# A hybrid encoder step on one core: adaLN weights by feature ahead of x, and the first three projection blocks begun on two thirds of the tokens

## The chip, the cores and the metric

The kernel runs on one core of one Trainium2 chip. The metric is device time in microseconds (us) of one launch. TensorE (PE) multiplies matrices and writes into PSUM, which has eight banks of 128 partitions by 512 float32. VectorE (DVE), ScalarE (ACT) and GpSimd (POOL) do the elementwise work, and SyncE (SP) issues nearly all transfers. Each engine works through its own instructions in the order in which the program wrote them.

## The reference

One layer of a streaming encoder is applied to 1024 prompt tokens and 32 sample tokens, 1056 tokens of 1024 features in all, each of the two sequences with its own conditioning vector c:

```
mod = silu(c) @ w_ada + b_ada                   # 6 x 1024 values; shift 1, scale 1 are the first 2048
h   = rmsnorm(x, g_mix) * (1 + scale1) + shift1
u   = h @ w_in                                  # 5640 columns: q, k, v of 8 heads x 64, the mLSTM's parts, gates
ya  = softmax(q k^T / 8 + rel_bias) v           # in bands of 64-token chunks; the sample also sees a cache
ym  = mlstm(conv(qm, km), vm, om, i, f)
x   = x + gate1 * ((sigmoid(ga) * (ya @ w_br_att) + sigmoid(gm) * (ym @ w_br_mlstm)) @ w_out)
x   = x + gate2 * swiglu(rmsnorm(x, g_ffn) * (1 + scale2) + shift2)
y   = rmsnorm(x, g_final)
```

Outputs are y and the new k, v, convolution and mLSTM states. All inputs are float32.

## The kernel before

Features lie on the partitions and tokens along the free dimension, in 8 tiles h[0..7] of 128 features by 1056 tokens. The tokens are cut into three tiles of 352. A float32 number is held as a rounded high part and the rest as a low part, and each product is three matmuls: weights high times h high, weights low times h high, weights high times h low (`PASSES`, line 41). One projection block is 128 columns of w_in: 3 token tiles x 8 feature tiles x 3 passes = 72 matmuls of 128x128 by 352 columns.

The stage that the change touches is the first one, up to the end of the first head pair's K, V and Q blocks. SP first issues eight tiles of x (128 tokens by 1024 features, 512 KB each, line 220), the sample's tokens, the first 2048 columns of w_ada in eight pieces of 128 rows (1 MB each, line 264), and then the first halves and second halves of two weight blocks, K and V (line 340). x comes token by token, so TensorE transposes it (`x_transposes`, line 281, evicted by ACT on line 282), and DVE sums the squares of each token (line 273). POOL takes the power -1/2 and the result is spread over the partitions as RB.

w_ada comes by rows, that is by the index that is summed over. The scale half of the product goes to TensorE (64 matmuls, line 322). The shift half is summed over rows on DVE (lines 312 and 314) and then over partitions on TensorE (`row_sums`, lines 348 and 352). No scale or shift is known before the last row of w_ada is in.

Then h is made feature tile by feature tile: `scaled_x` (DVE, x * scale * RB), `high_h` (ACT, adds the shift and rounds), `low_h` (DVE, the rest). `first_units` (line 467) runs the K and V blocks side by side over all three token tiles, one h tile after the other, in six PSUM banks, and Q follows as an ordinary block through `unit` (line 436, its matmuls are line 443). K is evicted by lines 553, 556 and 558, V by line 587, Q by lines 640 to 647. While Q runs, V is transposed back to tokens (`v_tail`, line 612) for the attention. After Q come the K, V and Q blocks of the second head pair, with the first pair's attention beside them; from there on the order of the program is the same before and after the change. The rotating pools that matter are `mm` (three PSUM banks), `ps` (psS and psT two banks each, psV one), and `wsp` (four tiles of split weights).

x is also written to a scratch tensor `xres` (line 1508) and read back for the residual. The relative-position bias is spread into a scratch tensor `rb_d` by a 3068 KB transfer (line 672) from which each head's tile is read.

## Time and profile before

| what | value |
|---|---|
| three runs, median | 1598.56 us (1597.11 to 1598.57) |
| profiled execution | 1597.75 us, its span 1596.1 us |
| TensorE busy | 1566.1 us, 98% of the span |
| first matmul of a projection block (line 475) | at 40.97 us |
| first matmul of the second head pair's K (line 443) | at 81.25 us |
| HBM read and written | 153.24 MB and 41.63 MB |

The span runs from the first to the last instruction. 1597.75 - 1596.1 = 1.65 us lie around it. Lines of the timeline give start, duration, engine, line, operation, output<-inputs, and in brackets the idle time of the engine before it and what ended that. Merged lines stand for several instructions in a row (x33).

### The profile page before, as it was taken

How to read it: one execution, taken by the hardware profiler on the slowest of the kernel's cores; microseconds unless marked ns; L12 is line 12 of the kernel's file. 1: busy time of each engine (PE TensorE's matmuls, PEld its weight loads, DVE VectorE, ACT ScalarE, POOL GpSimd, SP SyncE). 2: the span in 40 equal slices, each digit the busy share in tenths (PEclk: the TensorE clock that was granted, in tenths of full speed). 3: DMA queues.
4: the chain of work that ended last, by engine and by line, in shares of the span. 5: the costliest groups of instructions: out<-in, count | busy, mean ns of one | idle time of the engine just before them, and what ended most of it. 6: DMA issues, size and time to landing. Idle time of an engine off the chain costs nothing.

```text
span 1596.1 us, 27244 instructions
## 1 busy us (share of the span) xinstructions
PE 1566.1 (98%) x10167; PEld 1546.2 (97%) x10167; DVE 1126.4 (71%) x2291; ACT 790.5 (50%) x1735; POOL 420.0 (26%) x433
## 2 busy tenths in 40 slices
PE   7999999999999999999999999999999999999997
PEld 6989999999999999999999999999999999999997
DVE  7766555556776845546654699899888886799755
ACT  3665463544555545444433655544544444545443
POOL 0343242433222411000012100565565650000000
PEclk9999999999999999999999999999999999999999
DMA  9823323343132332675443311213222227427444
GB/s 364 265 83 94 98 82 109 86 135 110 43 94 67 88 86 75 133 257 176 133 145 112 106 54 54 95 57 103 81 80 94 68 78 252 143 80 249 130 136 155
DMA packets 209569, 193.48 MB, mean 121 GB/s; under 512 B 11530, under 2 KB 179118, under 8 KB 208414
## 3 DMA queue, kind: packets, MB, share of 16 engines
q1 hardware_dynamic: 206894, 189.92, 38.5%
q8 instruction: 80, 1.31, 0.4%
q10 hardware_dynamic: 2512, 1.77, 0.4%
q14 instruction: 51, 0.42, 0.1%
q0 software_dynamic: 32, 0.06, 0.0%
HBM read 153.24 MB, written 41.63 MB: 122 GB/s over the span
## 4 chain that ended last, share of the span: by engine, by line
PE 91%; DVE 3%; ACT 2%; DMA 2%; issue 1%; SPq 0%; POOL 0%; ACTq 0%; DVEq 0%; POOLq 0%
PE mm L443 41%; PE psb L1811 18%; PE mm L1811 11%; PE psb L2193 3%; PE mm L878 3%; PE mm L2193 2%; PE psV L783 2%; PE psb L2057 2%; PE psS L725 2%; PE psT L752 1%; DMA s<-in_w_ada_dram 1%; PE mm L2057 1%; DMA t<-in_x_sample_dram 1%; PE psV L1112 1%; PE mm L475 1%
## 5 line engine op out<-in xcount | busy, mean ns | idle before, releaser
L443 PE MATMUL mm<-s,wsp 128*128 128x352 f32 x4104 | 687.0, 324 | 0.0
L443 PEld LDWEIGHTS mm<-s,wsp 128*128 128x128 f32 x4104 | 657.3, 188 | 1.8 <-issue 0.4
L410 DVE TENSOR_TENSOR wsp<-wraw,wsp 128x512 fp32r<-128x512 f32 (+1 forms) x280 | 235.6, 858 | 114.1 <-ACT wsp L409 103.1
L1811 PE MATMUL psb<-s,wsp 128*128 128x352 f32 x1611 | 271.7, 322 | 1.6 <-DVE wsp L410 0.9
L409 ACT ACTIVATE wsp<-wraw 128x512 fp32r<-128x512 f32 x336 | 199.5, 617 | 142.4 <-PE psb L1811 44.5
L1811 PEld LDWEIGHTS psb<-s,wsp 128*128 128x128 f32 x1611 | 260.5, 188 | 2.1 <-DVE wsp L410 1.1
L1811 PE MATMUL mm<-s,wsp 128*128 128x352 f32 x933 | 159.3, 322 | 0.0
L1811 PEld LDWEIGHTS mm<-s,wsp 128*128 128x128 f32 x933 | 151.2, 188 | 0.5 <-DVE wsp L410 0.5
L745 POOL TENSOR_SCALAR st<-st,mx 128x640 f32<-128x640 f32 (+5 forms) x72 | 53.1, 738 | 186.2 <-DVE mx L744 171.2
L1207 DVE CUSTOM_DVE_ANT_0 junk<-wa,t 128x512 bf16<-128x512 f32 x128 | 94.7, 740 | 3.1 <-DMA wa<-in_w_mod_dram 2.1
L410 POOL TENSOR_TENSOR wsp<-wraw,wsp 128x512 fp32r<-128x512 f32 x56 | 74.9, 1357 | 57.1 <-ACT wsp L409 55.6
L739 DVE CUSTOM_DVE_ANT_0 st<-psS,bias 128x640 f32<-128x640 f32 (+5 forms) x72 | 44.5, 618 | 57.1 <-PE psS L725 41.9
L740 ACT ACTIVATE st<-st,mx 128x640 f32<-128x640 f32 (+5 forms) x72 | 47.9, 666 | 63.4 <-DVE mx L739 62.3
L1758 POOL TENSOR_TENSOR t<-t,sl 128x352 f32<-128x352 f32 x19 | 18.4, 969 | 212.8 <-ACT sl L1756 212.8
L759 ACT ACTIVATE pT<-psT 128x640 fp32r<-128x640 f32 (+3 forms) x80 | 38.7, 493 | 62.6 <-PE psT L752 47.6
L2166 POOL TENSOR_TENSOR fst<-fst,mhalf 128x6 f32<-128x6 f32 x1 | 2.3, 2312 | 221.1 <-DVE fst L2165 221.1
L764 DVE TENSOR_TENSOR pT<-psT,pT 128x640 fp32r<-128x640 f32 (+3 forms) x80 | 44.0, 558 | 22.2 <-ACT pT L759 22.2
L1420 POOL TENSOR_TENSOR wraw<-wraw,raw 128x512 f32<-128x512 f32 x33 | 55.8, 1705 | 0.9
L878 PE MATMUL mm<-s,s 128*128 128x264 f32 (+3 forms) x432 | 54.5, 283 | 0.0
L2193 PE MATMUL psb<-s,wsp 128*128 128x352 f32 x330 | 54.2, 324 | 0.0
L2193 PEld LDWEIGHTS psb<-s,wsp 128*128 128x128 f32 x330 | 53.1, 188 | 0.1
L878 PEld LDWEIGHTS mm<-s,s 128*128 128x128 f32 (+1 forms) x432 | 52.0, 179 | 0.5
(368 smaller groups left out, 2471.6 us busy)
## 6 DMA issues: line engine op xcount, KB each, us to landing
wraw<-in_w_in_dram SPq DMA_DIRECT2D x38, 512.0 KB, 4.0
wraw<-in_w_gate_up_dram SPq DMA_DIRECT2D x33, 512.0 KB, 3.9
wa<-in_w_mod_dram SPq DMA_DIRECT2D x64, 256.0 KB, 2.8
wraw<-in_w_down_dram SPq DMA_DIRECT2D x32, 512.0 KB, 4.3
a_d<-t SPq DMA_DIRECT2D x22, 528.0 KB, 2.7
g_d<-t SPq DMA_DIRECT2D x16, 528.0 KB, 3.2
x<-xres SPq DMA_DIRECT2D x16, 528.0 KB, 7.1
t<-g_d SPq DMA_DIRECT2D x16, 528.0 KB, 4.5
```

The lines of the kernel that those rows point to most:

```text
L409: act.activation(dst[:, 0], src, AF.Copy)
L410: eng.tensor_tensor(dst[:, 1], src, f(dst[:, 0]), op=ALU.subtract)
L443: pe.matmul(pt[:, :hi - lo], wt[(w0 + k) // 4][:, a, (w0 + k) % 4], xt[k][:, b, lo:hi], start=(k == 0 and q == 0), stop=(k == n - 1 and q ...
L739: dve.tensor_tensor_reduce(so, sv, bi, -1.0, 3.0e38, ALU.add, ALU.min, mx[:n, 1:2])
L740: act.activation(st[:n, :w], st[:n, :w], AF.Exp, bias=mx[:n, 1:2], scale=-1.0, accum_out=mx[:n, 2:3])
L745: pool.tensor_scalar(st[:n, :w], st[:n, :w], mx[:n, 3:4], 1.0, op0=ALU.mult, op1=ALU.mult)
L878: pe.matmul(pt[:n, :wd], hs[k][:, a, i * P:i * P + n], whl[b][:, k, :wd], start=(k == 0 and q == 0), stop=(k == KD - 1 and q == 2))
L1207: dve.tensor_tensor_reduce(junk, wa, crow[:, c], 1.0, 0.0, ALU.mult, ALU.add, at)
L1420: self.eng.tensor_tensor(a(dst), a(x), a(y), op=op)
L1811: pe.matmul(acc, wt[:, a, k], x[k][:, b], start=(start and not onto and k == 0 and q == 0), stop=(stop and k == 3 and q == 2), skip_group_ ...
L2057: pe.matmul(acc, wt[k // 4][:, u, k % 4], piece_of[k, i][:, v], start=(k == 0 and q == 0), stop=(k == KP - 1 and q == 2))
L2193: pe.matmul(acc, wt[(k - k0) // 4][:, u, (k - k0) % 4], piece_of[k, 2][:, v], start=(k == 0 and q == 0), stop=(k == NF - 1 and q == 2))
```

## The change

- **Layout.** The host hands over x transposed (features by tokens, prompt and sample joined), w_in as 44 blocks of 128 partitions by 1024 contiguous values, the eight gate columns apart, w_ada's first 2048 columns by output feature (piece j holds everything that scale and shift of feature tile j need), and the relative bias already spread. The transposes of x, the writes of x to `xres`, and the transfer into `rb_d` are gone; the residual reads x itself.
- **Order of the transfers.** Five of the eight pieces of w_ada come first, then x, but only its first 704 tokens, with the sixth piece after five of the eight feature tiles; then the seventh piece, first halves of K, V and Q weights, the eighth piece, the last 352 tokens of x, and the second halves.
- **adaLN.** All sums are on TensorE, 16 matmuls for each feature tile (`ada_sums`), and ACT adds bias and gain (`ada_done`).
- **Squares.** ACT squares x by feature tile, DVE adds the eight squares, TensorE sums over partitions (`token_sums`), POOL takes the power in two groups of three columns, TensorE and ACT spread it. The last 352 tokens follow on their own during the products of h[1] to h[4].
- **Products.** K, V and Q of the first head pair run side by side on the first two token tiles in six PSUM banks. Then K and V run on the last token tile in the two banks that are left, while ACT and DVE evict the six banks. Q's last token tile is an ordinary block. The cache, the bias tiles and the next three weight blocks are asked for earlier, and the empty steps between the three parts of V's way back to tokens are left out for this pair.

The core of the diff, where `put_k`, `put_v` and `put_q` are the evictions of the three blocks, cut out of their loops unchanged:

```
-    xtok = []
-
-    for i in range(KD):
-        if i % 2 == 0:
-            xt = slot([P, 2, D])
-            xtok += [xt[:, 0], xt[:, 1]]
-        sp.dma_start(xtok[i], xp[i * P:(i + 1) * P])
-    pool.dma_start(cols, params)
-    xsm = tmpt((TS, D))
-    sp.dma_start(xsm, xs_in)
...
+    act.dma_start(cols, params)
...
+    xTp = [slot([P, 2, T]) for _ in range(KD // 2)]
+    xTs = [xTp[j // 2][:, j % 2] for j in range(KD)]
+    CUT = TILES[2][0]
+    first_cols = (KA, VA, QA)
+    first_ws = [wraw.tile([P, KD, P], F32, tag="wraw", name=nm("wraw")) for _ in first_cols]
+    was = []
+
+    def in_block(c):
+        return w_in[(c - GA) // P + 28 if c >= GA else c // P]
+
+    def load_ada():
+        j = len(was)
+        wa = slot([P, 2, D])
+        for i in range(2):
+            sp.dma_start(wa[:, i], w_ada[i, j])
+        was.append(wa)
+
+    def load_first(half):
+        for raw, c in zip(first_ws, first_cols):
+            sp.dma_start(raw[:, 4 * half:4 * half + 4], in_block(c)[:, 4 * half:4 * half + 4])
+
+    sq2 = slot([P, 2, T])
+    for _ in range(5):
+        load_ada()
     for j in range(KD):
...
-    def load_ada(n):
-        while len(was) < n:
-            wa = slot([P, 2048])
-            sp.dma_start(wa, w_ada[len(was) * P:(len(was) + 1) * P, 0:2048])
-            was.append(wa)
-
-    load_ada(KD)
-
-    def square_sum(i):
-        n = P if i < 8 else TS
-        src = xtok[i] if i < 8 else xsm
-        junk = tmpt((P, D), BF16)
-        dve.tensor_tensor_reduce(junk[:n], src, src, 1.0, 0.0, ALU.mult, ALU.add, ssq[:n, i:i + 1])
...
+        if j == 5:
+            load_ada()
+        sp.dma_start(xTs[j][:, :CUT], x_t[j][:, :CUT])
+    load_ada()
+    load_first(0)
+    load_ada()
+    for i, xp in enumerate(xTp):
+        sp.dma_start(xp[:, :, CUT:], x_t[2 * i:2 * i + 2].rearrange("n p t -> p n t")[:, :, CUT:])
+    load_first(1)
...
-    def first_ada():
-        first_load()
-        for k in range(KD):
-            for b in range(KD):
-                out = psA[:, b * P:(b + 1) * P]
-                c = csil[:, k].unsqueeze(1).to_broadcast([P, DH, 2])
-                pe.matmul(out.rearrange("p (r c) -> p r c", c=2), was[k][:, D + b * P:D + (b + 1) * P], c,
-                          start=(k == 0 and b % 4 == 0), stop=(k == KD - 1), skip_group_check=True)
-            if k < KD - 1:
-                for c in range(2):
...
-    def first_units(ws):
-
-        S = ps_s()
-        pts = [[mmt() for _ in TILES], [S[:, :512], S[:, 512:], psA[:, :512]]]
-        wts = [w[3] for w in ws]
+    def first_units(put_k, put_v, put_q):
+
+        early, late = TILES[:2], TILES[2]
+        act.activation(silu1, ones, AF.Silu)
+        silu_cols()
+        for j in range(6):
+            pt = mmt()
+            ada_sums(j, 0, pt)
+            ada_sums(j, 1, pt)
+            if j < 3:
+                ada_done(j, pt)
+            else:
+                n = {3: 2, 4: 6, 5: KD}[j]
+                for i in range({3: 0, 4: 2, 5: 6}[j], n):
+                    square_sum(i, 0, CUT)
+                ada_done(j, pt)
+        token_sums(0, CUT, 0, DH)
+        groups = [(0, 3 * P), (3 * P, CUT)]
+        for i, (lo, hi) in enumerate(groups):
+            token_roots(i, hi - lo, 3 * DH * i, DH)
+        pt = mmt()
+
+        def spread(i):
+            lo, hi = groups[i]
+            bcast_cols(RB, roots[:, 1, 3 * i:3 * i + 3], [min(P, hi - a) for a in range(lo, hi, P)], lo)
...
+        ada_sums(6, 0, pt)
+        first_high(0, 0)
+        first_high(1, 0)
+        spread(0)
+        spread(1)
+        scaled_x(0, *early[0])
+        scaled_x(0, *early[1])
+        first_high(2, 0)
+        high_h(0, *early[0])
+        high_h(0, *early[1])
+        ada_sums(6, 1, pt)
+        ada_done(6, pt)
+        for i in range(3):
+            first_low(i, 0)
+        pts = [[mmt(), mmt()], [psS[:, :512], psS[:, 512:]], [psA[:, :512], mmt()]]
+        last = [tok, psH]
...
+        for t in range(2):
+            for i in range(3):
                 product(0, i, 0, t)
-            row_sums(0, t + 5, t + 6)
+        ada_sums(7, 0, psH)
+        ada_sums(7, 1, psH)
+        scaled_x(1, 0, CUT)
+        low_h(0, 0, CUT)
+        high_h(1, 0, CUT)
+        products(0, 1)
+        scaled_x(2, 0, CUT)
+        low_h(1, 0, CUT)
+        high_h(2, 0, CUT)
+        ada_done(7, psH)
+        products(0, 2)
+        for k in range(1, KD):
+            products(k, 0)
+            if k == 1:
+                for j in range(4):
+                    square(j, NT, *late)
+            if k + 2 < KD:
+                scaled_x(k + 2, 0, CUT)
+            if k + 1 < KD:
+                low_h(k + 1, 0, CUT)
+            if k + 2 < KD:
+                high_h(k + 2, 0, CUT)
+            if k == 1:
+                for j in range(4, 6):
+                    square(j, NT, *late)
+                for j in range(1, 4):
+                    add_square(j, NT)
+                first_high(0, 1)
+                first_low(0, 1)
...
+            products(k, 1)
+            if k == 3:
+                token_sums(late[0], NT, NT, 32)
+                token_roots(2, NT, NT, 32)
+                W.loaded = W.split_n = 3
+                W.load(6)
+                early_loads.append(cache_loads())
+                early_loads.extend(rel_bias_tile(h) for h in range(2))
+            if k == 4:
+                for i, n in enumerate((P, P, NT - 2 * P)):
+                    pe.transpose(tok[:, i * P:i * P + n], roots[:n, 1, 6 + i:7 + i].to_broadcast([n, P]), ident[:n, :n])
+                act.activation(RB[:, late[0]:late[1]], tok[:, :NT], AF.Copy)
+            for i in {5: (0, 1, 2), 6: (3, 4), 7: (5, 6)}.get(k, ()):
+                late_h(i)
+            products(k, 2)
+        for k in range(7, KD + 2):
+            late_h(k)
         for i in range(2):
...
+            put_k(*early[i], pts[0][i][:, :NT])
...
+            put_v(*early[i], pts[1][i][:, :NT])
+        for i in range(2):
+            put_q(*early[i], pts[2][i][:, :NT])
+        for k in range(KD):
+            for q in range(3):
+                for i in range(2):
+                    product(k, i, q, 2)
+        for i in range(3):
+            first[id(W.blocks[i])] = [None, None] + [p[:, :NT] for p in last[i:i + 1]]
+        for w, n in zip(W.blocks, (3, 3, 2)):
+            for _ in range(n):
                 W.used(w)
+        W.advance()
...
+    def square_sum(j, lo, hi):
+        n = hi - lo
+        o = sq2[:, j % 2, :n] if j else acc[:, :n]
+        act.activation(o, xTs[j][:, lo:hi], AF.Square)
+        if j:
+            dve.tensor_tensor(acc[:, :n], acc[:, :n], o, op=ALU.add)
+
+    def token_sums(a0, n, at, r):
+        for i, a in enumerate(range(0, n, P)):
+            b = min(a + P, n)
+            pe.matmul(tok[:b - a, at + r * i:at + r * (i + 1)], acc[:, a:b], ones[:, 0:1].to_broadcast([P, r]),
+                      start=(i == 0), stop=True, skip_group_check=True)
+
+    def ada_sums(j, part, pt):
+
+        for k in range(KD):
+            pe.matmul(pt[:, part * P:part * P + P].rearrange("p (r c) -> p r c", c=2),
+                      was[j][:, part, k * P:(k + 1) * P], csil[:, k].unsqueeze(1).to_broadcast([P, DH, 2]),
+                      start=(k == 0), stop=(k == KD - 1), skip_group_check=True)
+
+    def ada_done(j, pt):
+        act.activation(s1[:, :, j], pt[:, :2], AF.Identity, scale=gm1[:, j:j + 1], bias=gb1[:, j:j + 1])
+        act.activation(sh1[:, :, j], pt[:, P:P + 2], AF.Identity, bias=cols[:, R_ADA + j:R_ADA + j + 1])
+
+    def scaled_x(j, lo, hi):
+        for c, a, b in col_segments(lo, hi):
+            x = xTs[j][:, a:b]
+            if c == 0:
+                dve.scalar_tensor_tensor(x, x, s1[:, 0, j:j + 1], RB[:, a:b], op0=ALU.mult, op1=ALU.mult)
+            else:
+                pool.tensor_tensor(x, x, RB[:, a:b], op=ALU.mult)
+
```

How instructions stand on three engines before and now. First SP, where the transfers are asked for; s is a large tile (x or w_ada), wraw a raw weight block. Before, from the last two pieces of w_ada on:

```order
L264 DMA s_126<-in_w_ada_dram 128x2048
L264 DMA s_128<-in_w_ada_dram 128x2048
L340 DMA wraw_294<-in_w_in_dram 128x4x128
L340 DMA wraw_295<-in_w_in_dram 128x4x128
L340 DMA wraw_294<-in_w_in_dram 128x4x128
L340 DMA wraw_295<-in_w_in_dram 128x4x128
L419 DMA wraw_300<-in_w_in_dram 128x8x128
L672 DMA rb_d<-in_rel_bias_dram 1024x1x767
```

Now, from the fifth piece of w_ada on (s_103 to s_135 are pieces of w_ada, s_95 to s_98 pairs of feature tiles of x):

```order
L249 DMA s_115<-in_w_ada_dram 128x1024 x2
L262 DMA s_95<-in_x_dram 128x704 x2
L262 DMA s_96<-in_x_dram 128x704 x2
L262 DMA s_97<-in_x_dram 128x704
L249 DMA s_123<-in_w_ada_dram 128x1024 x2
L262 DMA s_97<-in_x_dram 128x704
L262 DMA s_98<-in_x_dram 128x704 x2
L249 DMA s_129<-in_w_ada_dram 128x1024 x2
L254 DMA wraw_99<-in_w_in_dram 128x512
L254 DMA wraw_100<-in_w_in_dram 128x512
L254 DMA wraw_101<-in_w_in_dram 128x512
L249 DMA s_135<-in_w_ada_dram 128x1024 x2
```

The first weights stand behind all of x and w_ada before; now they stand behind seven pieces of w_ada and two thirds of x.

Second, TensorE from the end of the K and V products on. Before (mm_723 and mm_755 are Q's first two token tiles, mm_766 the first transpose of V, t_708 V itself):

```order
L443 MATMUL mm_723<-s_621,s_631 128x352 x3
L443 MATMUL mm_723<-s_658,s_631 128x352 x3
L443 MATMUL mm_755<-s_432,s_631 128x352 x3
L443 MATMUL mm_755<-s_480,s_631 128x352 x3
L443 MATMUL mm_755<-s_514,s_631 128x352 x3
L612 MATMUL mm_766<-ident,t_708 128x128 x4
L443 MATMUL mm_755<-s_541,s_631 128x352 x3
```

Now (psT_150 and psV_151 are K and V on the last token tile, mm_756 Q's last token tile, t_668 V, mm_767 and mm_780 the transposes):

```order
L475 MATMUL psT_150<-s_550,wsp_328 128x352
L475 MATMUL psV_151<-s_550,wsp_331 128x352
L402 MATMUL mm_756<-s_347,s_345 128x352 x3
L402 MATMUL mm_756<-s_390,s_345 128x352 x3
L402 MATMUL mm_756<-s_400,s_345 128x352 x3
L674 MATMUL mm_767<-ident,t_668 128x128 x4
L402 MATMUL mm_756<-s_422,s_345 128x352 x3
L402 MATMUL mm_756<-s_451,s_345 128x352 x3
L674 MATMUL mm_780<-ident,t_668 128x128 x4
L402 MATMUL mm_756<-s_483,s_345 128x352 x3
```

Before, 33 matmuls of Q stand between V's last product and its first transpose; now nine do.

Third, ACT around the evictions (s_682 and s_657 are K, t_708 and t_668 V, t_672 and s_671 Q, wsp a split weight block). Before:

```order
L386 ACTIVATE s_658<-s_598,sh_270 128x1024
L385 ACTIVATE s_598<-s_598,sh_270 128x32
L386 ACTIVATE s_658<-s_598 128x32
L553 ACTIVATE s_682<-mm_426 64x352 x2
L553 ACTIVATE s_682<-mm_427 64x352 x2
L556 ACTIVATE kf_683<-mm_427 128x192
L553 ACTIVATE s_682<-mm_428 64x352 x2
L556 ACTIVATE kf_683<-mm_428 128x352
L409 ACTIVATE wsp_698<-wraw_629 128x512
L409 ACTIVATE wsp_699<-wraw_629 128x512
L587 ACTIVATE t_708<-psS_425 128x352 x2
L587 ACTIVATE t_708<-psT_267 128x352
```

Now:

```order
L348 ACTIVATE s_550<-s_98 128x32
L601 ACTIVATE s_657<-mm_363 64x352 x2
L601 ACTIVATE s_657<-mm_364 64x352 x2
L604 ACTIVATE kf_658<-mm_364 128x192
L642 ACTIVATE t_668<-psS_152 128x352 x2
L702 ACTIVATE t_672<-psT_150 128x352
L704 ACTIVATE s_671<-psT_150 64x352 x2
L702 ACTIVATE t_672<-mm_365 128x352
L704 ACTIVATE s_671<-mm_365 64x352 x2
L364 ACTIVATE wsp_740<-wraw_497 128x512
L364 ACTIVATE wsp_741<-wraw_497 128x512
L601 ACTIVATE s_657<-psT_150 64x352 x2
```

The evictions of K, V and Q on two token tiles now stand together behind the last late h tile, and the split of the next weight block stands between them and the evictions of K and V on the last token tile.

371 lines of the change are left out of this document (161 added, 210 removed).

## The prediction

> **What bounds the kernel now.** I read the page first: the busy table, the chain of work that ended last, and of the transfers the row of the weight blocks (KB each, median us from issue to landing).
>
> ```profile
> PE 1566.1 (98%) x10167; PEld 1546.2 (97%) x10167; DVE 1126.4 (71%) x2291; ACT 790.5 (50%) x1735; POOL 420.0 (26%) x433
> ...
> PE 91%; DVE 3%; ACT 2%; DMA 2%; issue 1%; SPq 0%; POOL 0%; ACTq 0%; DVEq 0%; POOLq 0%
> ...
> wraw<-in_w_in_dram SPq DMA_DIRECT2D x38, 512.0 KB, 4.0
> ```
>
> TensorE is the bound. The kernel gets shorter only if TensorE stands idle less or does less, and 30 us of idle time are all there is. Next the timeline of TensorE, to see where they lie.
>
> ```profile
> 4.59 0.45 PE L281 MATMUL mm<-ident,s 128*128 128x128 f32 x1 [4.59 <-DMA s<-in_x_prompt_dram]
> ...
> 25.78 2.05 PE L322 MATMUL psT<-csil,s 128*128 128x128 f32 x16 [1.21 <-DMA s<-in_w_ada_dram]
> ...
> 35.86 2.05 PE L322 MATMUL psT<-csil,s 128*128 128x128 f32 x16 [0.54 <-DMA s<-in_w_ada_dram]
> 37.75 1.67 PE L348 MATMUL psV<-ones,t 128*128 128x64 f32 x14
> ...
> 40.97 0.43 PE L475 MATMUL mm<-s,wsp 128*128 128x352 f32 x1 [0.66 <-ACT s L386]
> ...
> 48.29 0.75 PE L475 MATMUL mm<-s,wsp 128*128 128x352 f32 x3 [0.42 <-DVE s L392]
> ...
> 68.52 5.55 PE L443 MATMUL mm<-s,s 128*128 128x352 f32 x33
> 73.90 0.60 PE L612 MATMUL mm<-ident,t 128*128 128x128 f32 x4
> ...
> 81.25 6.05 PE L443 MATMUL mm<-s,wsp 128*128 128x352 f32 x36
> ```
>
> The first projection matmul starts at 40.97 us. Until then TensorE does only preparation and waits for transfers. From 48.29 to 68.52 us 126 matmuls take 20.2 us, 0.161 each; from 68.52 to 73.90 us 33 take 5.4 us, 0.163 each. So from 48 us on TensorE runs without a gap. At 81.25 us the second head pair's K begins, and behind that point the order of the program stays as it was. The gain or loss is therefore how much earlier or later that point comes.
>
> What the start waits for is told by the waits of TensorE in the first 66 us and by the windows of the transfers (last two columns: busy share of the 16 DMA engines, GB/s).
>
> ```profile
> PE mm L281 <- DMA s<-in_x_prompt_dram: 6.7, 4, 4.6
> PE psT L322 <- DMA s<-in_w_ada_dram: 3.1, 5, 1.2
> ...
> 4.00:6.00 2.00, 0.66 (x2) 0.40 (x3) 1.40 (x3) 0.00 (x0) 0.00 (x0) 1.00 1.02 407
> ...
> 28.00:30.00 2.00, 1.72 (x15) 1.72 (x16) 1.98 (x3) 0.00 (x0) 0.00 (x0) 1.00 1.01 418
> ...
> 36.00:38.00 2.00, 2.00 (x19) 2.00 (x20) 1.77 (x4) 1.01 (x2) 0.00 (x0) 1.00 1.17 290
> ```
>
> The transfers are full from 4 us on (share above 1). x comes in runs of 4 KB at 407 GB/s, w_ada in runs of 8 KB at 418, the first weights in runs of 512 B at 290. All 12.72 MB of x and w_ada must be in before the first product.
>
> **When the bytes land now.** The fourth piece of w_ada (8.52 MB with all of x) ends a wait at 25.78 us, the eighth (12.72 MB) at 35.86: 0.416 MB/us, as if from 5.3 us on. With runs of 4 KB and 2816 B instead of 8 KB I take 0.40 as the lower bound. Ahead of the last early piece of x stand six pieces of w_ada (6.29 MB) and 2.88 MB of x, 9.18 MB: between 27.3 and 28.2 us, I take 27.8. The first halves of the K, V and Q weights then land at 31.0, 31.7 and 32.3, the eighth piece of w_ada at 34.9, the rest of x at 38.4, the second halves by 40.4.
>
> **From the last x to the first product.** The prices are from the groups of the first 90 us by shape (busy, mean ns).
>
> ```profile
> L375 DVE SCALAR_TENSOR_TENSOR s<-s,s,t 128x1024 f32<-128x1024 f32 x6 | 7.6, 1274 | 0.0
> ...
> L465 DVE TENSOR_TENSOR wsp<-wraw,wsp 128x512 fp32r<-128x512 f32 x4 | 2.6, 680 | 0.0
> L375 DVE SCALAR_TENSOR_TENSOR s<-s,s,t 128x352 f32<-128x352 f32 x4 | 2.2, 578 | 0.1
> ...
> L365 DVE TENSOR_TENSOR s<-psT,cols 128x16 f32<-128x16 f32 x1 | 0.2, 174 | 0.2 <-PE psT L322 0.2
> ...
> L386 ACT ACTIVATE s<-s,sh 128x1024 fp32r<-128x1024 f32 x6 | 6.9, 1153 | 4.4 <-DVE s L375 3.1 <-DVE sh L360 0.7 <-DMA xres<-s 0.6
> L553 ACT ACTIVATE s<-mm 64x352 fp32r<-64x352 f32 x8 | 3.7, 457 | 4.0 <-PE mm L475 3.6 <-PE mm L443 0.4
> ...
> L461 ACT ACTIVATE wsp<-wraw 128x512 fp32r<-128x512 f32 x4 | 2.4, 623 | 15.6 <-DMA wraw<-in_w_in_dram 15.6
> ...
> L640 ACT ACTIVATE t<-mm 128x352 f32<-128x352 f32 x3 | 1.4, 467 | 1.1 <-PE mm L568 1.1
> ...
> L556 ACT ACTIVATE kf<-mm 128x192 f32<-128x192 f32 x1 | 0.3, 330 | 0.0
> ...
> L1138 POOL TENSOR_TENSOR dn<-dn,mhalf 128x2 f32<-128x2 f32 x16 | 12.1, 759 | 1.3
> ...
> L394 POOL TENSOR_TENSOR s<-s,s 128x32 fp32r<-128x32 f32 x8 | 4.7, 592 | 38.2 <-ACT s L386 36.6 <-DMA xres<-s 1.7
> ...
> L1588 POOL TENSOR_TENSOR rs<-rs,mhalf 128x4 f32<-128x4 f32 x3 | 3.2, 1081 | 19.5 <-DVE rs L1586 19.5
> ```
>
> By length, 704 columns cost DVE 0.94 us (0.86 back to back, where the next one starts 0.08 earlier) and ACT 0.83; a power of three columns lies between 0.76 and 1.08, so 0.92. From 27.8 us: square 0.83 on ACT, add 0.94 on DVE, six sums 0.7 (0.12 each, line 348), 0.2 on DVE, the power 0.92: 31.4. Three transposes 0.4: 31.8. ACT rounds K's and V's weights ahead of the copy into RB, until 32.3, then copies: 32.8. scaled_x 0.58, and behind Q's weights (0.62) high_h 0.59: the first product at **34.5 us**, 6.5 us earlier than now. The second power and copy run beside this.
>
> **From there to the second pair's K.** TensorE has 216 matmuls of 352 columns as before, 35.0 us at 0.162; the eighth piece of w_ada 1.9 (35.86 to 37.75); three sums and three transposes 0.7; nine transposes of V 1.0. Without a wait: 34.5 + 38.6 = 73.1 us.
>
> Waits: (a) DVE works through three weight remainders, squares of the late tokens and h, 16.4 us in all ahead of the remainder of h[4], from 32.8 us: 49.2. Behind it stand the late roots and a power (1.2): 50.4. TensorE asks for them after 84 products, the eighth piece and the sums, at 34.5 + 13.6 + 2.2 = 50.3. About 0.3 with the hand-over. The rest of DVE's list (five operations of 704, sixteen of 320) ends at 61.6; TensorE wants the last of it at 68. (b) V's transposes. Behind K's last product ACT splits half a weight block (0.62), evicts K's last tile (1.38) and V's (0.47): 2.5 us. TensorE meanwhile has nine matmuls, 1.5 us: a wait of 0.9 that before was covered by 33. The six banks' evictions before it (4 x 0.457, 0.33, 4 x 0.467, 4 x 0.457: 5.9) run from 61.1 to 67.0 us, under the 7.8 us of the last tiles of K and V, and hide.
>
> (c) TensorE after a pause. Its very first matmuls, in two windows of line 281:
>
> ```profile
> L281 PE MATMUL mm<-ident,s x6: 421/421/421, 6.3 to 7.3; 128*128 128x128 f32 x6
> ...
> L281 PE MATMUL mm<-ident,s x11: 272/273/323, 9.3 to 10.4; 128*128 128x128 f32 x11
> ```
>
> Until about 8.2 us, 3.6 us after its first one, a matmul takes 421 ns and starts every 0.2 us; then 272, every 0.1. The granted clock reads 1.00 throughout. In the changed kernel TensorE has one piece of w_ada (1.9 us) between about 19 and 29 us, so it may start the products at that pace. 3.6 us then hold 11 products instead of 22: 1.8 us at most, 0 at least; I take 1.2, since some of that time falls on sums and the eighth piece.
>
> The Trainium skill says the same ("TensorE: Matmul & The Clock Gate", Part 1: The HAM clock gate): after an idle window of about 3.4 us the array runs at half its clock until it has been busy for such a window. The trace agrees with 3.6 us. By that rule alone the term would be 1.8 and the forecast 0.6 later.
>
> Sum: 73.1 + 0.3 + 0.9 + 1.2 = 75.5 us against 81.25, 5.75 us earlier. The profiled execution took 1597.75 us (span 1596.1 and 1.65 around it), 0.81 under the median of the three runs, so: 1597.75 - 5.75 = **1592.0 us**.
>
> At nothing: the writes of x, the transfer into the scratch of the bias and the 512 B runs of later weights, since TensorE waits for no transfer after 36 us and its work covers them (the sum of any exposed one would be its landing time, 4.0 us for a weight block). ACT issues the small parameters, well ahead of the first w_ada piece (5.3 + 1.05 / 0.40 = 7.9 us). SP's load of c waits for RB's buffer (free at 62 us) with a weight load behind it; three blocks of weights are in by then.
>
> **Rivals.**
>
> *All hidden (best case).* The fast rate, matmuls every 0.16 us throughout, no wait for V: 34.0 + 38.6 = 72.6 us, 8.65 earlier, **1589.1**. For it: TensorE is warm after 3.6 us at about 60% busy. Against: there is no such stretch between 19 and 34 us.
>
> *Short runs bind.* x now comes in 2816 B pieces of rows 4224 B apart. If these go at the 290 GB/s of the 512 B runs, 2.88 MB take 9.9 us instead of 7.0 and all behind it is 2.9 later: **1594.9**. Against: 4 KB runs lose only 3% on 8 KB ones (407 against 418). The Trainium skill ("DMA: Bandwidth & Descriptors", Specifications) puts the smallest transfer for line rate at 512 B, by which this rival is worth nothing; the window at 290 disagrees with it, though the bias transfer shares that window.
>
> *Evictions pile up (the other side).* The late h tiles give POOL sixteen operations of 32 columns, 9.5 us by line 394. These rows show DVE beside POOL.
>
> ```profile
> 54.63 1.44 DVE L375 SCALAR_TENSOR_TENSOR s<-s,s,t 128x1024 f32<-128x1024 f32 x2
> ...
> 61.10 4.60 DVE L392 SCALAR_TENSOR_TENSOR s<-s,sh,s 128x1024 fp32r<-128x1024 f32 x2
> ...
> 55.14 0.87 POOL L394 TENSOR_TENSOR s<-s,s 128x32 fp32r<-128x32 f32 x1 [2.88 <-ACT s L386]
> ...
> 61.09 3.52 POOL L410 TENSOR_TENSOR s<-wraw,s 128x512 fp32r<-128x512 f32 x2
> ```
>
> Beside POOL's 512-column subtractions DVE took 4.60 us for two operations, instead of 2.5 (two of 1.27). If it stood still for all 9.5 us, its list would end at 71.1, the evictions at 77.0, the split and the last tiles of K and V at 80.0; TensorE would then do 15 matmuls and the transposes (3.4): 83.4, 2.2 later than now, **1599.9**. It decides only if ACT gets to the evictions after 69 us, 8 us behind my reckoning. Against: beside a 32-column operation (55.14) DVE kept its 1.44.
>
> **How the numbers follow.** Forecast 0.55 (its own range 1590.2 to 1594), best case 0.17, short runs 0.16, pile-up 0.07, and 0.05 that something later gives the gain back. A measurement here tells about 0.2% (3.2 us, 1595.4 to 1601.8) from no change. Faster: 0.54 + 0.17 + 0.09 = 0.80; same 0.15; slower 0.05. The range 1588.8 to 1596.5 leaves out about 0.05 below and 0.12 above.
>
> **What would show it.** The first 352-column product at 34 to 35 us; its first dozen starting every 0.3 us or every 0.16; the last early x at 27 to 28.5; the second pair's K at 75 to 76 us; waits of TensorE of about 1 us for V, and little else between. I am wrong if the start comes after 38 us, if TensorE waits long for ACT behind K's and V's last tiles, or if it loses more around the first scores than it does now.

## The result, and the profile after

The change makes the kernel a little slower: 1601.06 us (median of 22 runs, 1599.80 to 1601.88) against 1598.7 us for the kernel before on the same chip (22 runs, 1597.11 to 1600.51 without a single one of 2575.86). The ratio is 1.0014, with a 95% interval of 1.0008 to 1.0021. The forecast was 1592.0, so the change went the other way. The profiled execution took 1600.62 us, its span 1598.9, 2.8 us more than the span before.

The busy table of the page says that TensorE is still the bound, with 3.5 us more of busy time (1566.1 before):

```profile
PE 1569.6 (98%) x10197; PEld 1552.4 (97%) x10197; DVE 1104.7 (69%) x2276; ACT 793.8 (50%) x1748; POOL 418.0 (26%) x439
```

Where it was lost is seen at the point that the prediction named, the first matmul of the second head pair's K (line 402 now, 443 before). It moved from 81.25 to 83.88 us, later by 2.6, though the first projection matmul moved from 40.97 to 35.38, earlier by 5.6. Between these two points there are 48.5 us instead of 40.3, 8.2 more; 3.5 of them are the eighth piece of w_ada, which now lies there. Here is the timeline of TensorE after the change; a number in brackets is the idle time ahead of the row and what ended it.

```profile
4.85 23.77 PE L321 MATMUL mm<-csil,s 128*128 128x128 f32 x192 [4.85 <-DMA s<-in_w_ada_dram]
29.35 1.56 PE L304 MATMUL psT<-ones,t 128*128 128x64 f32 x12 [0.73 <-DVE t L299]
...
35.38 0.41 PE L475 MATMUL mm<-s,wsp 128*128 128x352 f32 x1
...
36.49 3.73 PE L321 MATMUL psV<-csil,s 128*128 128x128 f32 x32
...
52.20 0.43 PE L475 MATMUL psT<-s,s 128*128 128x352 f32 x1 [1.09 <-DVE roots L315]
...
64.48 0.32 PE L475 MATMUL mm<-s,s 128*128 128x352 f32 x1
68.53 0.66 PE L475 MATMUL psT<-s,wsp 128*128 128x352 f32 x1 [3.73 <-ACT s L704]
...
73.97 0.39 PE L475 MATMUL psT<-s,wsp 128*128 128x352 f32 x1
...
83.88 6.03 PE L402 MATMUL mm<-s,wsp 128*128 128x352 f32 x36
```

Three things stand there. Six pieces of w_ada keep TensorE busy from 4.85 to 28.6 us without a gap, 3.6 us for each at full pace, and the eighth piece takes from 36.49 to the next product at 39.98, 3.5 us; the prediction had 1.9. ScalarE, which takes up each piece when its sums are done, has the same 3.6 us from one to the next (17.94 to 21.51):

```profile
17.94 0.35 ACT L326 ACTIVATE s<-mm,gb,cols 128x2 f32<-128x2 f32 x1 [3.07 <-PE mm L321]
...
21.51 0.35 ACT L326 ACTIVATE s<-mm,gb,cols 128x2 f32<-128x2 f32 x1 [1.71 <-PE mm L321]
```

The first matmul of K's last token tile waits 3.73 us for ScalarE. And behind that pause TensorE is slow, as the windows of TensorE show (length, busy time and the number of matmuls that ran in the window, then the granted clock, the transfers' share and GB/s):

```profile
5.00:30.00 25.00, 24.27 (x198) 1.00 1.03 406
...
65.00:69.00 4.00, 0.47 (x2) 0.78 0.11 39
69.00:74.00 5.00, 5.00 (x19) 0.50 0.00 0
74.00:79.00 5.00, 5.00 (x33) 0.99 0.01 3
```

From 69 to 74 us the clock is 0.50 and 19 matmuls run, from 74 to 79 it is 0.99 and 33 run. From 68.53 to 73.97 a matmul takes 0.293 us where it takes 0.161 otherwise. These 5.44 us hold 18 matmuls, and the first behind a pause counts as one and a half: 5.44 - 18.5 x 0.161 = 2.45 us lost.

What ends the long wait is told by ScalarE's timeline in the same stretch.

```profile
64.40 1.86 ACT L601 ACTIVATE s<-mm 64x352 fp32r<-64x352 f32 x4
66.27 0.33 ACT L604 ACTIVATE kf<-mm 128x192 f32<-128x192 f32 x1
66.50 0.81 ACT L642 ACTIVATE t<-psS 128x352 f32<-128x352 f32 x2
67.19 0.48 ACT L702 ACTIVATE t<-psT 128x352 f32<-128x352 f32 x1
67.53 0.95 ACT L704 ACTIVATE s<-psT 64x352 fp32r<-64x352 f32 x2
```

ScalarE evicts K (601, 604), V (642), then Q's first tile (702, 704), and TensorE goes on when Q's first tile has been read, at 68.5. K's last tile isn't written where Q's first one stands: the two have one half each of the two-bank tile psT (`psA[:, 512:]`, called `tok`, and `psA[:, :512]`). TensorE waited for the reader of the other half.

Behind 84 us the profile is as before. The wait of the first scores for VectorE grew from 0.86 to 1.35 us, the next one is 1.74 as it was.

### The profile page after: what moved, and what is told of

Read it like the earlier page. It is cut to its first block, busy times and chain, and to the rows that moved or that the text cites. A ratio compares the mean times of both kernels' runs of the same rounds, so it can differ in the third digit from the quotient of the medians.

```text
span 1598.9 us, 27295 instructions
## 1 busy us (share of the span) xinstructions
PE 1569.6 (98%) x10197; PEld 1552.4 (97%) x10197; DVE 1104.7 (69%) x2276; ACT 793.8 (50%) x1748; POOL 418.0 (26%) x439
## 4 chain that ended last, share of the span: by engine, by line
PE 90%; ACT 4%; DVE 3%; DMA 2%; issue 1%; POOL 0%; ACTq 0%; SPq 0%; DVEq 0%; POOLq 0%
PE mm L402 40%; PE psb L1869 18%; PE mm L1869 10%; PE psb L2251 3%; PE mm L946 3%; PE mm L2251 2%; PE psV L851 2%; PE psb L2115 2%; PE psS L792 1%; PE psT L819 1%; PE mm L2115 1%; DMA s<-in_w_ada_dram 1%; DMA s<-in_x_dram 1%; PE psV L1180 1%; PE psT L1182 1%
```

## The experiments

Theory A says, in three parts: (1) a write to one half of psT waits for the readers of the other half; (2) the pause halves TensorE's clock for some us; (3) a piece of w_ada costs 3.6 us of TensorE, since a float32 product shows as two instructions (x192 for 96 products). The rivals were that ScalarE's evictions set the end wherever the bank is, and that the slow stretch comes from late operands.

### V's last tile first

```diff
-        for k in range(KD):
-            for q in range(3):
-                for i in range(2):
+        for i in (1, 0):
+            for k in range(KD):
+                for q in range(3):
                     product(k, i, q, 2)
```

> V's 24 products of the last tile stand ahead of K's 24, instead of one of each in turn; nothing else moves. V's bank is free, K's is one half of the two-bank tile whose other half holds Q's first tile. Theory A (K's last tile waits for ScalarE's reads of Q's half, and TensorE is slow after that pause): 24 x 0.161 = 3.9 us of V's products fill the 3.73 us, the wait falls under 0.3 us and no matmul after it takes 0.29 us; the second head pair's K begins about 3.73 + 2.45 = 6.2 us earlier, at 77.7, and the time is about 1594.9. Rival B (the evictions themselves set the end, the wait moves behind): the wait turns up again before Q's last tile or the second pair's K, the time stays within 1 us of 1601.1. Rival C (the pause costs, the slow pace has another cause, such as late operands): 3.7 us less, about 1597.3, with 18 matmuls at 0.29 us still there.

Measured: 1596.13 us (1594.62 to 1596.39), ratio to before 0.9983 (0.9974 to 0.9992), 4.9 us less than after the change. The row of the second pair's K in the timeline, then the windows of TensorE:

```profile
77.75 6.03 PE L402 MATMUL mm<-s,wsp 128*128 128x352 f32 x36
```

```profile
69.00:74.00 5.00, 5.00 (x33) 1.00 0.01 3
```

The wait is gone and the clock stays at 1.00. The second pair's K begins at 77.75, 6.1 us earlier, as theory A had it (77.7). The span falls by 4.5 us, not 6.2: the missing 1.7 is a stretch at half clock far behind this stage, at 425 us, and has its own section below.

### Work in the pause

```diff
+        for _ in range(23):
+            pe.matmul(psH[:, :NT], W.blocks[1][3][0][:, 0, 0], hs[0][:, 0, late[0]:late[1]], start=True, stop=True)
         for k in range(KD):
```

> 23 products that nobody reads go into V's free bank in the stretch in which TensorE waits for K's bank (23 x 0.161 = 3.7 us); V's first real product overwrites them. The wait for the bank stays, TensorE is merely busy in it. Theory A (the slow pace is the consequence of the pause): the 48 products behind take 0.161 us each from the first, 2.45 us less, about 1598.6; the release of K's bank stays at 68.5 us. Rival C (late operands or the evictions that run beside them): they keep 0.29 us for about 18 matmuls, time within 0.6 us of 1601.1. If the added products merely delay: above 1601.1.

Measured: 1599.36 us (1598.29 to 1601.08), 1.7 less than after the change. Here the bank is no sooner free, TensorE just has something to do, as its timeline and its windows show:

```profile
65.08 3.87 PE L557 MATMUL psV<-s,wsp 128*128 128x352 f32 x23
```

```profile
69.00:74.00 5.00, 5.00 (x31) 1.00 0.00 0
```

31 matmuls run between 69 and 74 us instead of 19, at a clock of 1.00, and the second pair's K begins at 81.78, 2.1 us earlier. With the same operands and the same neighbours the slow stretch is gone: it follows from the pause. Of the 6.2 us, 3.7 are thus the wait and about 2.1 to 2.4 its consequence.

### Another tile in the shared bank pair

```diff
-        pts = [[mmt(), mmt()], [psS[:, :512], psS[:, 512:]], [psA[:, :512], mmt()]]
+        pts = [[psA[:, :512], mmt()], [psS[:, :512], psS[:, 512:]], [mmt(), mmt()]]
```

> The tiles trade banks: K's first tile stands in the shared two-bank tile, Q's first in a bank of its own; the order of all work stays. ScalarE evicts K's first tile first, so theory A (a write to one half waits for the reads of the other) has K's last tile wait for 64.4 + 0.93 us of ScalarE and 1.06 us of VectorE, until about 66.4 instead of 68.5: a wait of 1.6 us, 2.1 us less, about 1599.0; and if a pause of 1.6 us leaves TensorE at its pace, 2.45 us less again, 1596.5. Rival B (K's last tile waits until all six evictions are done or for VectorE's low parts of h): the wait stays at 3.7 us and the time at 1601.

Measured: 1600.4 us (1598.85 to 1600.81). TensorE's waits in the timeline, and its windows:

```profile
52.37 0.43 PE L475 MATMUL psT<-s,wsp 128*128 128x352 f32 x1 [1.82 <-DVE roots L315]
57.94 0.43 PE L475 MATMUL psT<-s,wsp 128*128 128x352 f32 x1 [0.55 <-ACT t L544]
69.25 0.40 PE L475 MATMUL psT<-s,wsp 128*128 128x352 f32 x1 [1.39 <-DVE s L606]
```

```profile
50.00:55.00 5.00, 3.18 (x17) 0.77 0.61 210
55.00:60.00 5.00, 4.45 (x26) 0.89 0.01 2
```

The late wait is 1.39 us (1.6 was expected), ends with VectorE's reading of K's first tile, and leaves the clock alone: part (1) of theory A again, on a mere renaming of banks. But the time hardly falls. One reason is that K's first tile now meets the late sums in the other half twice, at 52.37 and at 57.94. K's product comes first of the six, so it waits longer than Q's did (1.82 against 1.09), and this pause halves the clock for 3.4 us. The second pair's K still begins at 82.06, 1.8 us earlier than after the change. The other reason is that this profile has a second stretch at half clock, from 107.3 to 110.7 us, which the profile of the kernel after the change doesn't have; it takes about 1.7 us back.

### The late sums apart, alone with V first, and then all three

V first stands in both kernels as above, and the two helpers that make the sums and roots take the tile as an argument.

```diff
...
-                token_sums(late[0], NT, NT, 32)
-                token_roots(2, NT, NT, 32)
+                token_sums(late[0], NT, NT, 32, psH)
+                token_roots(2, NT, NT, 32, psH)
...
-                    pe.transpose(tok[:, i * P:i * P + n], roots[:n, 1, 6 + i:7 + i].to_broadcast([n, P]), ident[:n, :n])
-                act.activation(RB[:, late[0]:late[1]], tok[:, :NT], AF.Copy)
+                    pe.transpose(psH[:, i * P:i * P + n], roots[:n, 1, 6 + i:7 + i].to_broadcast([n, P]), ident[:n, :n])
+                act.activation(RB[:, late[0]:late[1]], psH[:, :NT], AF.Copy)
```

> V's last tile ahead of K's as before, and the late token sums and their three transposes go into V's free bank instead of K's half of the shared tile. Theory A (the shared two-bank tile is the cause of the 1.1 us wait of Q's products for VectorE's reading of the late sums too): that wait goes, second head pair's K begins at 76.6 instead of 77.7, 1.1 us less than the 1596.1 of the run with V first, 1595.0; less by up to 1.7 more, 1593.3, where no later pause falls into one window of TensorE's clock. Rival (the products behind would wait for the late roots anyway): the wait turns up at the three transposes or at the late products, 1596.1 again.

Measured: 1596.33 us (1594.28 to 1600.87), no gain on V first alone, and the spread is nearly four times as wide. The profiled execution is the longest of the 11 (span 1599.2). Rows of its timelines: TensorE, ScalarE, GpSimd, and last GpSimd in the kernel after the change and in the kernel with three edits that follows.

```profile
70.83 6.91 PE L475 MATMUL psT<-s,wsp 128*128 128x352 f32 x24 [3.00 <-ACT s L704]
```

```profile
58.96 0.41 ACT L347 ACTIVATE s<-s,sh,s 128x32 f32<-128x32 f32 x1 [2.26 <-POOL s L337]
```

```profile
54.91 4.44 POOL L337 TENSOR_TENSOR s<-s,t 128x32 f32<-128x32 f32 x3 [1.15 <-ACT t L544]
```

```profile
55.58 1.18 POOL L337 TENSOR_TENSOR s<-s,t 128x32 f32<-128x32 f32 x3 [1.87 <-ACT t L544]
```

```profile
54.92 1.77 POOL L337 TENSOR_TENSOR s<-s,t 128x32 f32<-128x32 f32 x3 [1.15 <-ACT t L544]
```

The 1.1 us wait at 52 us went, as expected. But GpSimd's three small products for the sample's tokens begin 0.7 us earlier, while VectorE still works on 704 columns, and take 4.44 us instead of 1.18. ScalarE waits 2.26 us for them, its evictions end later, and K's bank is awaited for 3.0 us again. Why they take so long is open. The early start beside VectorE isn't enough: in the kernel with three edits they begin at 54.92 beside the same operation of VectorE and take 1.77. Only this longest execution was profiled, so it isn't shown either that this delay is what spreads the times.

The remedy tried is to make K's bank depend on the first eviction instead of the fifth. The third kernel has V first, the sums apart and the banks traded as above.

> Three edits together: V's last tile ahead of K's, the late sums and transposes in V's free bank, and K's first tile instead of Q's in the shared two-bank tile. Theory A (the false dependency between the two halves of that tile is all that held TensorE between 50 and 70 us): all waits there go except up to 0.5 us for the late roots; second head pair's K at 76.6 in each execution, since K's first tile is read out by 66.4 at the latest 68.7 and its bank is wanted at 67.7; 1595.0, and not the two groups (1594.3 to 1595.7 and 1596.3 to 1600.9) of the pair without the trade of banks. Rival (ScalarE's list of late h, held by GpSimd's 128x32 products, sets the end whatever the bank): the median stays at 1596.3 with the same spread.

Measured: **1594.98 us** (1593.27 to 1596.82), ratio to before 0.9979 (0.9970 to 0.9988): faster than both kernels. The timeline has the K where it was expected, and the longest waits of TensorE from 28 to 135 us are these (in total, times, longest):

```profile
76.57 6.03 PE L402 MATMUL mm<-s,wsp 128*128 128x352 f32 x36
```

```profile
PE psV L851 <- ACT pT L826: 1.7, 1, 1.7
PE psS L792 <- DVE mx L806: 1.4, 1, 1.4
PE psT L304 <- DVE t L299: 1.0, 1, 1.0
PE psV L543 <- POOL roots L316: 0.4, 1, 0.4
```

Theory A's waits are gone, but not its steady time: the 11 runs lie at 1593.3 to 1593.6, 1594.7 to 1595.2 and 1596.2 to 1596.8, a spread of 3.6 us where V first alone had 1.8. Steps of 1.2 to 1.6 us are near the 1.7 us of a stretch at half clock (below); only the shortest run was profiled, and it has none, so that isn't shown.

### Columns of the adaLN sums

Each product of the sums streams 128 columns, 64 copies of the two conditioning columns, and only two are read. Two kernels stream fewer.

```diff
-            pe.matmul(pt[:, part * P:part * P + P].rearrange("p (r c) -> p r c", c=2),
-                      was[j][:, part, k * P:(k + 1) * P], csil[:, k].unsqueeze(1).to_broadcast([P, DH, 2]),
+            pe.matmul(pt[:, part * P:part * P + 2],
+                      was[j][:, part, k * P:(k + 1) * P], csil[:, k],
```

> The adaLN sums stream 2 columns instead of 128 (64 copies of 2), of which only 2 were read; the 16 weight tiles of a piece stay. Theory A1 (a float32 product is two instructions of about 0.115 us whatever its columns: the six token sums with 64 and the three with 32 columns cost the same for each): a piece stays at 3.6 us, the first product at 35.4, time 1601 within 1. Rival A2 (the price goes by the columns): a piece falls under 1 us, the eighth piece gives back 2.5 us and the first product comes at about 34.5; 1598 or less, unless the wait for K's bank takes it back.

> The kernel after the change with 32 columns (16 copies of 2) in the adaLN sums instead of 128. With 2 columns a piece took 7.1 us at a granted clock of one half. Theory H (TensorE's clock is granted by how much it streams in a window, not by its instructions being back to back; 128 columns are just enough): 32 columns leave it at half as 2 did, a piece takes about 7 us and the time is near 1629. Rival (any 32 columns are enough): a piece takes 3.6 us and the time is 1601.

Measured, one run each: 1628.95 us with 2 columns and 1626.81 with 32. Both theories of the first run were wrong, and the one of the second, made after it, held. The timeline of the kernel with 2 columns and its windows:

```profile
5.18 41.12 PE L321 MATMUL mm<-csil,s 128*128 128x2 f32 x192 [5.18 <-ACT csil L282]
...
57.28 0.64 PE L475 MATMUL mm<-s,wsp 128*128 128x352 f32 x1
```

```profile
57.00:72.00 15.00, 15.00 (x61) 1.00 0.01 2
72.00:80.00 8.00, 8.00 (x54) 1.00 0.54 195
```

A product becomes dearer with fewer columns: 41.1 us for the 96 products of six pieces, 0.43 each, against 0.25 with 128 (23.77 us, the slow start included; 0.22 at full pace). TensorE is never idle, yet works at about half pace until 72 us: even the 352-column products take 0.29 us up to there and 0.16 behind. So instructions back to back didn't raise the pace here; with 32 columns they streamed too little, with 128 enough. The 126 columns that nobody reads thus keep TensorE at full pace. Nor do they set a product's price: at half pace it is 0.43 us with 2, 32 and 128 columns alike (the first 4 us after the change, a start every 0.21 us and two per product). In this stretch the granted clock reads 1.00, so that column doesn't show a clock that has never yet risen; the spacing of the matmuls does. The trace bears that out in another way: its first record of the clock stands at 71.97 us here and at 69.54 with 32 columns, where the pace rises, and between 8.3 and 11.0 us in the other eleven profiles.

### Half of the sums, and no eighth piece

With V first, every piece sums half of its contraction.

```diff
-        for k in range(KD):
+        for k in range(4):
             pe.matmul(pt[:, part * P:part * P + P].rearrange("p (r c) -> p r c", c=2),
...
-                      start=(k == 0), stop=(k == KD - 1), skip_group_check=True)
+                      start=(k == 0), stop=(k == 3), skip_group_check=True)
```

> With V first, each adaLN piece sums half of its contraction (8 products instead of 16, so the output is wrong): 1.8 us a piece, under the 2.7 us in which a piece is transferred. Theory P (TensorE's 3.6 us a piece set the start): the first product comes at 34.6 instead of 35.4 and the eighth piece takes 1.8, second head pair's K 2.6 us earlier, at 75.1. Theory G (less work leaves pauses while x is transferred, between about 19 and 24 us, and the clock is then at half): the sums, transposes and first products run at half pace, the first product comes at 36.5 or later and products take 0.29 us for the first 3.4 us or more, so that the K begins no earlier than 77.

Measured, one run: 1594.9 us. Theory P is out, and theory G's mechanism held, with smaller effect than it said: the first product came at 36.05 instead of 36.5 or later, and the first projection products were at full pace again. Timeline and windows:

```profile
22.32 3.75 PE L321 MATMUL mm<-csil,s 128*128 128x128 f32 x16 [4.72 <-DMA s<-in_w_ada_dram]
...
36.05 0.43 PE L475 MATMUL mm<-s,wsp 128*128 128x352 f32 x1 [0.43 <-ACT s L345]
```

```profile
20.00:28.00 8.00, 3.75 (x16) 0.55 1.03 406
28.00:35.00 7.00, 6.61 (x30) 0.54 1.04 389
```

With less to do TensorE pauses 4.72 us while x is transferred, its clock falls to half, the token sums and transposes take twice as long, and the first projection matmul comes at 36.05 us, later than with all sums. The second pair's K begins at 78.07, 0.3 later than with V first alone, though half of the sums are gone. That the time is nevertheless 1.2 us below that of V first alone comes from behind this stage: this profile has no stretch at half clock there, the one of V first has one.

The other kernel leaves the eighth piece's sums out altogether, in two forms. In the first one its shift and scale are read from the seventh's PSUM tile where the eighth's stood.

```diff
-        ada_sums(7, 0, psH)
-        ada_sums(7, 1, psH)
...
-        ada_done(7, psH)
+        ada_done(7, pt)
```

> With V first, the sums of the eighth piece are left out (its shift and scale are read from the seventh's, so the output is wrong). It prices that piece on TensorE. Prediction's figure: 1.9 us. Theory A (a float32 product is two instructions, 16 products are 32 instructions): 3.5 us; second head pair's K begins at 74.2 instead of 77.7, unless ScalarE's late list holds it and the gain turns into a wait for the late h (then about 1 to 2 us of it stay).

That run (1596.95 us) measured something else: the tile was held until then, and TensorE waited 4.18 us for it. The second form reads them at once.

```diff
         ada_done(6, pt)
+        ada_done(7, pt)
...
-        ada_sums(7, 0, psH)
-        ada_sums(7, 1, psH)
...
-        ada_done(7, psH)
```

> With V first, the sums of the eighth piece are left out, and its shift and scale are read from the seventh's right behind that one's, so that no bank is held longer (the output is wrong). Prediction's figure for the piece: 1.9 us of TensorE. Theory A (16 float32 products are 32 instructions): 3.5 us, second head pair's K at 74.2 to 74.5 instead of 77.7; where ScalarE's late list does not move with it, a wait for K's bank takes up to 3 us of it back.

Measured, one run: 1597.86 us; the K begins at 79.55, 1.8 us later than with V first alone, though 16 products are gone. Rows of TensorE's timeline:

```profile
48.86 0.80 PE L304 MATMUL psT<-ones,t 128*128 128x32 f32 x6 [1.18 <-DVE t L292]
51.92 0.66 PE L476 MATMUL psT<-s,s 128*128 128x352 f32 x1 [1.54 <-DVE roots L315]
```

TensorE now stands at VectorE's sums of the late tokens (1.18) and roots (1.54), and the clock is at half from 50.7 to 57.6 us (and from 105.4 to 108.8 once more). With two short waits (0.43 and 0.20) TensorE idles 2.3 us more here than with V first alone, whose wait at this place was 1.08, and of the 5.65 us from 51.92 to 57.57 at half clock it loses half, 2.8. Together they are more than the 3.5 us that were spared. Between 33.8 and 64.5 us VectorE is busy for 29.0 of 30.7 us after the change, TensorE for 29.6. So the expectation was wrong, and no wait for K's bank came in its place: the piece costs TensorE 3.5 us, but its removal isn't worth them, since VectorE sets the pace a little behind and the new pauses halve the clock.

### One kernel, two profiles

V first was profiled once more.

> The kernel with V first once more, unchanged, for a second profile. In the first one TensorE's granted clock is halved for 3.41 us behind the 2.0 us pause that ends at 424.3, and the kernel after the change has the same pause without it. Theory G (the clock is judged over windows of 3.41 us whose phase differs from one execution to the next, so a pause of 1.7 to 2.0 us halves the clock only where one window holds nearly all of it): other places have it this time, or none, and the span changes by 1.7 us for each; 1594.4 less 1.7 is 1592.7 with none. Rival (the place follows from the program): the drop stands at 424.9 again and the span at 1594.4 within 0.3.

Measured: 1597.9 us, span 1596.2, against 1594.4 in the first profile; the K begins at 78.0. First the pause and the clock in the first profile, then the clock in the second.

```profile
424.26 0.74 PE L819 MATMUL psT<-ident,st 128*128 128x128 f32 x5 [2.01 <-DVE pT L831]
```

```profile
424.50:425.00 0.50, 0.50 (x6) 0.87 0.00 0
425.00:428.00 3.00, 3.00 (x13) 0.50 0.37 90
428.00:428.50 0.50, 0.50 (x4) 0.72 0.00 0
```

```profile
100.00:110.00 10.00, 7.97 (x45) 0.83 0.03 11
420.00:430.00 10.00, 8.00 (x49) 0.87 0.07 27
430.00:440.00 10.00, 10.00 (x69) 0.96 0.19 56
```

The first profile has one stretch at half clock, the second has two, and its span is 1.8 us longer. The added drop, between 100 and 110 us, stands at the 1.74 us wait of line 851, which cost nothing more in the first profile and in that of the kernel after the change. The drop behind 424 us came back, which the rival expected; that there is another one, the rival can't explain. The kernel after the change has the same 2.0 us pause without any drop. Its row, and the windows in which its clock falls at 67 us and rises at 74:

```profile
430.19 0.74 PE L819 MATMUL psT<-ident,st 128*128 128x128 f32 x5 [2.00 <-DVE pT L831]
```

```profile
67.00:67.50 0.50, 0.00 (x0) 0.76 0.00 0
...
74.00:74.50 0.50, 0.50 (x4) 0.91 0.00 0
```

A mean of 0.87 in a row of 0.5 us means 0.13 us at half clock, one of 0.72 means 0.28. So in the first profile the clock is at half from 424.87 to 428.28, which is 3.41 us. After the change it is at half from 67.26 to 74.09, twice 3.41. The next fall there, when the work runs out, is at 1593.02, 445 steps of 3.413 us behind 74.09. With such steps counted back, 67.26 and 74.09 lie at the same phase (2.41 us), and the borders next to the pause that ends at 430.19 are at 429.07 and 432.48: the pause lies 0.88 us before and 1.12 behind a border. In the first profile of V first all of its 2.01 us lies between the borders 421.46 and 424.87. So this pause of 2.0 us halves the clock of the next window if one window holds it, and costs half of 3.41, 1.7 us; if a border splits it, it costs nothing more. The same pause stands in all thirteen profiles: in three of them a window holds 1.98 us of it or more, and these have the drop; in the ten others, with at most 1.87 in one window, it is missing.

For shorter pauses the length alone doesn't decide. The 1.74 us wait of line 851 lies wholly within one window in the first profile of V first (100.60 to 104.01) and did nothing there; without the eighth piece it also does, and halved the clock. Counting all idle time of TensorE in each window at full clock up to the end of the work, 1.93 us or more always halved the clock in these profiles and 1.47 or less never did; of ten windows in between, five were followed by half clock (1.54, 1.74, 1.79, 1.81 and 1.82 us idle) and five were not (1.60, 1.73, 1.74 and twice 1.87). What else counts is open. Since streaming few columns left the pace at half in the runs above, the work in the rest of the window is a candidate.

The Trainium skill ("TensorE: Matmul & The Clock Gate", Part 1: The HAM clock gate) gives a free-running window of 3413 ns, and that agrees with 3.41. It has the clock fall after an idle window of about 3.4 us; here a window with 1.5 to 2.0 us of idle time was enough in several places, and the measurement decides.

## Why the prediction was wrong, point by point

**The bound, and the place where it is decided: right.** The second pair's K came 2.63 us later and the span grew by 2.8. Nothing that was costed at nothing behind that point shows up (bias, weights, writes of x).

**Transfers: right.** The squares of the last two early tiles begin at 26.5 us on ScalarE without a wait between them, so x was in by 27.3, where 27.3 to 28.2 was forecast. x and w_ada moved at 406 GB/s, so the rival of short runs (290) is out. The smallest transfer for line rate of the Trainium skill ("DMA: Bandwidth & Descriptors", Specifications), 512 B, agrees with that, as the runs of x are 2816 B long; runs of 512 B weren't tried here on their own.

**From the last x to the first product: 34.5 forecast, 35.38 measured.** The six token sums took 1.5 us instead of 0.7, and the second half of the seventh piece stands right ahead of the product. Both are the error of the next point.

**The eighth piece: 1.9 forecast, 3.5 measured; this term was mis-sized.** The row of the kernel before that gave 1.9 (x16) holds the 8 products of the scale half of a piece, two instructions each. The changed kernel's piece holds 16 products. The same slip made the prologue look idle. TensorE has 3.6 us for each piece, so it was busy up to 28.6 us and had no long pause in which to cool: **the argument of (c)**, one piece of 1.9 us between 19 and 29 us, was false, and the start lost nothing to the clock: the sums are slow for their first 4 us, but the token sums behind them then still wait 0.73 us for VectorE. The run with half of the sums has such a pause, of 4.72 us; its first product came 1.5 us later than theory P had it, where (c) allowed 1.2, and the loss fell on the sums and transposes, not on the products.

**(a) The late roots: 0.3 forecast, 1.09 measured,** for another reason. Not the transposes waited but Q's product in the other half of psT, for VectorE's reading of the sums. With the sums in another bank the transposes waited 0.4, close to the forecast.

**(b) Evictions that hide under the last tiles: this is the step that failed.** The prediction compared lengths, 5.9 us of evictions against 7.8 us of matmuls, and didn't ask into which bank the first of these matmuls writes. It writes into the half of a tile whose other half is the fifth of six to be evicted, so nothing hid: 3.73 us. ScalarE also came to the evictions 3.3 us later (64.4 instead of 61.1), behind its own list of late h, but the last products of K's early tiles start at 63.67 and end at about 64.1, so they could have begun at most some 0.3 us sooner. The forecast wait of 0.9 us for V's transposes didn't come.

**(c) TensorE after a pause: the mechanism right in kind, place and size off.** It struck behind this wait, 2.45 us instead of 1.2 at the start. The 3.6 us were also misread: in the kernel before, a matmul of line 281 that starts at 8.61 still takes 421 ns and the pace rises at about 9.1, which is 4.5 us after the first matmul at 4.59 and 3.3 after the second at 5.78. And a pause doesn't need to last a whole window of 3.4 us, as shown above.

By steps: the start 0.9, the eighth piece 1.6, the late roots 0.8, V's transposes -0.9, the bank 3.7 and the clock 1.2 more than forecast make 7.3 of the 8.4 us between 75.5 and 83.88; about 1 us is spread over the sums and transposes and wasn't traced. With the waits for the shared bank gone, in the kernel with three edits, K begins at 76.57 us and the time is 1594.98: inside the forecast range, 3 us above its centre. It comes so close partly by luck: the eighth piece cost 1.6 us more than forecast, V's transposes 0.9 and the clock 1.2 less.

**The rivals.** The one on the other side put its price on GpSimd slowing VectorE, with a point of 69 us for ScalarE to reach the evictions. The sign came true, but not by that mechanism: ScalarE was there at 64.4. A relative of it, GpSimd held up beside VectorE, appeared only in the profile with the late sums apart, and its cause is open. By the prediction's own bounds for no change, 1595.4 to 1601.8, 1601.06 still counts as the same, to which it gave 0.15, and a gain, to which it gave 0.80, is out; 22 runs put the time just above the kernel before. No case among the rivals asked what each PSUM write waits for.

## What to carry to other kernels

When evictions are to run under later matmuls, go by banks, not by sums of time: for each first write after the change, name the tile that it lands in, all readers of that tile (also of a half that the write doesn't touch) and their place in the evicting engine's list. Count a pause of TensorE with its consequence: here one of 3.7 us cost 2.4 more, one of 2 us cost 1.7 more or nothing, depending on where it fell. Independent work in the pause took the consequence away, and another order of two blocks the pause itself. So before work is taken off an engine that looks too busy, look for the pauses that it leaves: half of the sums less, or one piece less, brought K no earlier here. And before a row is used as a price, check how many instructions one operation of the program makes in it.

## What the runs showed that was not expected

- TensorE's pace depends on what it streams, not only on whether it is busy: with 2 or 32 columns per product, back to back, it stayed at half pace for over 60 us, and 28 and 26 us were lost.
- The granted clock read 1.00 throughout that stretch; it showed drops, but not a clock that had never risen.
- The same kernel differs by 1.8 us between two profiles, which is one more stretch of 3.41 us at half clock. For the pause of 2.0 us its place in the windows decides; for that of 1.74 us something else does too.
- Three GpSimd products of 32 columns took 1.18, 1.77 or 4.44 us, the last two from the same start beside the same work of VectorE.
